# Hybrid decoder layer on one core: a turn between the gate rows' diagonal tiles and their matmul, three merged chunks turned on VectorE through DRAM, and read-backs issued by ScalarE

## The chip, the core and the metric

The kernel runs on one core of a Trainium2 chip. The metric is the device time of one execution in microseconds (us), here the median of several runs. The core has TensorE (PE, matmuls; its weight loads are listed apart as PEld), VectorE (DVE), ScalarE (ACT), GpSimd (POOL) and SyncE (SP), each with an instruction queue of its own that it works off in order. DMAs are issued from a queue and run beside the engines.

## What is computed

One layer of a decoder for 256 tokens of width 2048, all in float32:

```python
h = rmsnorm(x, ln_g);  proj = h @ w_in + b_in            # w_in: 2048 columns in, 14 groups of columns out
ml_out  = head_layernorm(mlstm(conv_silu(q,k), v, i, f)) * sigmoid(o) * silu(z)   # 6 heads
rt_out  = head_layernorm(retention(rope(q), rope(k), v)) * silu(z)                # 6 heads
xa_out  = softmax(q @ mk.T / 16) @ mv * silu(z)          # 4 heads, mk and mv from rmsnorm(mem) @ w_mem_kv
merged  = g0 * (ml_out @ w_br_ml) + g1 * (rt_out @ w_br_ret) + g2 * (xa_out @ w_br_xa)   # g = sigmoid(gate columns)
out     = rmsnorm(x + merged @ w_out, final_g)
```

The two gates `i` and `f` of the mLSTM (6 heads each) come from 12 columns of `w_in`. From them a small piece of work, called gate rows below, makes the running sums and maxima that the mLSTM needs.

## The kernel before

All weights pass once through the core in 1 MB tiles `raw` (128 x 2048), three buffers of them (`NRAW`), loaded by SP (`dma`, L212 to L239). Each half tile is a **unit**. For a unit ScalarE rounds the half to the matmul's reduced format (`wh`, L268) and VectorE takes the remainder (`wl`, L269); the products are three matmuls per block, high by high, high by low and low by high (L909 to L911), 12 matmuls of 512 columns in a unit. `wh` and `wl` have four buffers each (`NSPLIT`). The main loop (L932 to L944) writes, for each unit i: the splits up to unit i + 3 (`LA` = 3), the products of unit i, what is due at the end of a chunk of columns (`finish`), and then one turn of background work (`bg.step`, L125).

A cast for unit i + 3 therefore waits until PE has ended unit i - 1, whose buffer it takes, and PE needs it three units later.

**Background jobs** are Python generators. A `yield` ends a turn; `yield n` also lets the job rest for n further turns. Two jobs at most are begun, and awake ones take turns in rotation. The order that comes out is the program's order on each engine; nothing is scheduled at run time. So a turn's place is fixed by the number of yields ahead of it.

The places that the change touches:

- `gate_rows_job` (L384 to L444) begins after the 12 gate columns' products (L864, L865). Its first turn makes two 128 x 128 diagonal tiles on VectorE (L392) from the row norms, multiplies a tile of ones with each on PE (L393), which spreads the norms over all partitions, and copies the product (L395).
- `swapped` (L455 to L470) turns tiles of 128 x 512 by blocks: VectorE transposes 32 x 32 blocks (L463), four DMAs write the result to DRAM (L466), one DMA reads it back in the other order (L468), all issued by SP. Between write and read stands `yield 3`, between read and use `yield 2`. Users are `transposes_job` (10 times, two tiles, copy L476) and `out_transposes` (16 times, one tile, L526 to L531), 26 in all.
- `merge_job` (L699 to L713), one for each of four chunks of `merged`, transposes a chunk with eight 128 x 128 transposes on PE (L706) into two PSUM banks, from which ScalarE and VectorE make the high and low parts (L711, L712) that the output projection reads.

Of the kernel before, what the change touches and what calls it, by code (L numbers as in the profile page):

```python
# [12 lines left out]
ALU = mybir.AluOpType  # L13
# [3 lines left out]
P = 128  # L17
D = 2048
T = 256
# [131 lines left out]
def body(ctx, tc, A, out):  # L151
    nc = tc.nc
    V, S, G, PE = nc.vector, nc.scalar, nc.gpsimd, nc.tensor
# [6 lines left out]
    def til(tag, shape, dt=F32, bufs=1):  # L160
        names[tag] = names.get(tag, 0) + 1
        return sb.tile(shape, dt, tag=tag, name=f"{tag}_{names[tag]}", bufs=bufs)

    def bank(tag="bg", bufs=4):
        names[tag] = names.get(tag, 0) + 1
        return pp.tile([P, 512], F32, tag=tag, name=f"{tag}_{names[tag]}", bufs=bufs)

    def stage(w=512):
        return til("st", [P, 512], bufs=4)[:, :w]

    def f32(ap):
        return ap.bitcast(F32)
# [26 lines left out]
    ones = til("ones", [P, P])  # L199
# [48 lines left out]
    def part(w):  # L248
        off[0] += w
        return cst[:, off[0] - w:off[0]]  # L250
# [3 lines left out]
    bif, freq, ident, mask = part(1), part(64), part(P), part(P)  # L254
# [6 lines left out]
    rms = {n: til("r_" + n, [P, 2]) for n in ("mem", "x")}  # L261
# [122 lines left out]
    def gate_rows_job(psif):  # L384
        rows = iter(range(8))
        R = lambda: scr[:, next(rows), :]
        RT = R()
        G.memset(RT, 0.0)
        rb = bank()
        for tb in range(2):  # L390
            dg = stage(128)
            V.tensor_scalar(dg, ident, rms["x"][:, tb:tb + 1], None, op0=ALU.mult)  # L392
            PE.matmul(rb[:, tb * P:(tb + 1) * P], lhsT=ones, rhs=dg, start=True, stop=True)  # L393
        rbs = R()
        S.copy(rbs, rb[:, :T])  # L395
        fi = R()[:38]
        S.copy(fi, psif[64:102, :T])
        V.tensor_tensor(fi, fi, psif[:38, :T], op=ALU.add)
        V.tensor_tensor(fi, fi, rbs[:38], op=ALU.mult)
        V.tensor_scalar(fi, fi, bif[:38, 0:1], None, op0=ALU.add)  # L400
        yield
        f = fi[:6]
        ti = R()[:6]
        V.tensor_copy(ti, fi[32:38])
        e = R()[:6]
        V.scalar_tensor_tensor(e, f, -1.0, f, op0=ALU.mult, op1=ALU.max)
        S.activation(e, e, AF.Exp, bias=0.0, scale=-1.0)
        u = R()[:6]
        V.tensor_scalar(u, e, 1.0, None, op0=ALU.add)
        ln = R()[:6]  # L410
        S.activation(ln, u, AF.Ln)
        V.tensor_scalar(u, u, 1.0, None, op0=ALU.subtract)
        V.tensor_tensor(e, e, u, op=ALU.subtract)
        yield
        V.tensor_tensor(ln, ln, e, op=ALU.add)
        lf = u
        V.scalar_tensor_tensor(lf, f, 0.0, ln, op0=ALU.min, op1=ALU.subtract)
        b = R()[:6]
        for tb in range(2):
            sl = slice(tb * P, (tb + 1) * P)  # L420
            V.tensor_tensor_scan(b[:, sl], ones[:6], lf[:, sl], 0.0, op0=ALU.mult, op1=ALU.add)
        a = RT[:6]
        V.tensor_tensor(a, ti, b, op=ALU.subtract)
        yield
        zero = rbs
        G.memset(zero, 0.0)
        G.tensor_copy(MT, zero)
        V.tensor_tensor(sel, ident[:, 0:6], ident[:, 32:38], op=ALU.add)
        M = zero[:6]
        V.tensor_tensor_scan(M[:, :P], a[:, :P], a[:, :P], 0.0, op0=ALU.max, op1=ALU.max)  # L430
        mp = til("mp", [P, 1])[:6]
        V.tensor_tensor(mp, b[:, P - 1:P], M[:, P - 1:P], op=ALU.add)
        V.tensor_tensor_scan(M[:, P:], a[:, P:], a[:, P:], mp, op0=ALU.max, op1=ALU.max)
        V.tensor_scalar(RT[32:38, :P], a[:, :P], b[:, P - 1:P], None, op0=ALU.add)
        V.scalar_tensor_tensor(RT[64:70], b, -1.0, M, op0=ALU.mult, op1=ALU.subtract)
        V.tensor_copy(MT[:6], M)
        V.tensor_tensor(MT[32:38], M, f32(MT[:6]), op=ALU.subtract)
        yield
        ps = bank()
        for tb in range(2):  # L440
            PE.transpose(ps[:, tb * P:(tb + 1) * P], RT[:, tb * P:(tb + 1) * P], ident)
        S.copy(cT.rearrange("p a b -> p (a b)"), ps[:, :T])
        S.activation(enm, cT[:, :, 64:70], AF.Exp)
        yield  # L444
# [5 lines left out]
    outT = {}  # L450
# [4 lines left out]
    def swapped(us):  # L455

        n = len(us)
        x, y = (til(t, [P, 8 * P], bufs=2)[:, :4 * n * P].rearrange("p (a c) -> p a c", a=4) for t in ("tx", "ty"))  # L460
        d = dr.tile([4, 32, 4, n * P], F32, tag=f"td{n}", name=f"td{n}_{names['tx']}", bufs=2)
        for u in range(n):
            V.transpose(x[:, :, u * P:(u + 1) * P].rearrange("p b (c i) -> p c b i", i=32),  # L463
                        us[u].rearrange("p (c b j) -> p c b j", b=4, j=32))
        for a in range(4):
            nc.sync.dma_start(d.rearrange("b j a c -> a j b c")[a], x[32 * a:32 * a + 32])  # L466
        yield 3
        nc.sync.dma_start(y.rearrange("p a c -> p (a c)"), d.rearrange("b j a c -> (b j) (a c)"))  # L468
        yield 2
        return y  # L470

    def transposes_job(us, dst, off=0):

        yield
        y = yield from swapped(us)
        S.copy(dst[:, :, off:off + T].rearrange("p g (t a i) -> p g t a i", a=4, i=32),  # L476
               y.rearrange("p a (t g i) -> p g t a i", t=2, i=32))
        yield
# [39 lines left out]
    def out_transposes(o, h, g):  # L518

        y = yield from swapped([o])  # L520
        for db in range(2):
            k = 2 * h + db
            src = y.rearrange("p a (t d i) -> p d t a i", t=2, d=2)[:, db]
            hv, lv = (out_part(n, k)[:, 0].rearrange("p (t a i) -> p t a i", t=2, a=4) for n in "hl")
            if g is None:
                S.copy(hv, src)  # L526
                V.tensor_tensor(lv, src, f32(hv), op=ALU.subtract)
            else:
                S.activation(hv, src, AF.Copy, bias=0.0, scale=g[:, k:k + 1])
                for tb in range(2):  # L530
                    V.scalar_tensor_tensor(lv[:, tb], src[:, tb], g[:, k:k + 1], f32(hv)[:, tb],  # L531
                                           op0=ALU.mult, op1=ALU.subtract)
# [141 lines left out]
    merged = [None]  # L674
# [23 lines left out]

    def merge_job(c):  # L699

        yield
        us = [merged[0][:, c, tb, :] for tb in range(2)]
        ps = [bank(), bank()]
        for j in range(4):
            for tb in range(2):
                PE.transpose(ps[j // 2][:, (j % 2) * T + tb * P:(j % 2) * T + (tb + 1) * P],  # L706
                             us[tb][:, j * P:(j + 1) * P], ident)
        for i in range(2):
            h = outT["mh"][:, 4 * c + 2 * i:4 * c + 2 * i + 2, :].rearrange("p a t -> p (a t)")
            l = outT["ml"][:, 4 * c + 2 * i:4 * c + 2 * i + 2, :].rearrange("p a t -> p (a t)")  # L710
            S.copy(h, ps[i])  # L711
            V.tensor_tensor(l, ps[i], f32(h), op=ALU.subtract)  # L712
        yield  # L713
# [5 lines left out]
    def finish(ci, ps, bias, tbs=(0, 1)):  # L719
# [73 lines left out]
        elif kind == "br":  # L793
# [10 lines left out]
            if b == 1 and c:  # L804
                mjobs.append(bg.add(merge_job(c)))
# [45 lines left out]
    def products(i, u):  # L851
# [5 lines left out]
        if e[0] == "if":  # L857
            if hf == 0:
                psums[ci] = [bank()]
            ps = psums[ci][0]  # L860
            for k in range(8):
                kt = hf * 8 + k
                a = wh[:, k * P:(k + 1) * P]
                PE.matmul(ps[:, :T], lhsT=a, rhs=aTh[:, kt, :], start=kt == 0, stop=False)  # L864
                PE.matmul(ps[:, :T], lhsT=a, rhs=aTl[:, kt, :], start=False, stop=kt == NKT - 1)  # L865
            if hf == 1:
                jobs["rows",] = bg.add(gate_rows_job(ps))
            return
# [4 lines left out]
        if k0 == 0:  # L873
            load_bias(ci)
            if wname.startswith("w_br"):
                bg.finish(core_jobs[{"w_br_xa": "x", "w_br_ml": "m", "w_br_ret": "r"}[wname]])
            psums[ci] = [bank("d0", 2), bank("d1", 2)]
            if kind == "br" and idx == (1, 1):
                outT["mh"] = til("aTh", [P, NKT, T], F32R)
                outT["ml"] = til("aTl", [P, NKT, T], F32R)  # L880
                mjobs.append(bg.add(merge_job(0)))
# [151 lines left out]
```

## Time and profile before

| what | us |
|---|---|
| median of three runs | 1231.35 |
| lowest and highest run | 1230.87, 1232.48 |
| the profiled execution, its own time | 1233.26 |
| span of its instructions | 1231.3 |
| TensorE busy | 1217.9 (99%) |
| VectorE busy | 768.7 (62%) |
| ScalarE busy | 589.4 (48%) |
| GpSimd busy | 141.4 (11%) |

The page gives, from top to bottom, each engine's busy time, the span in 40 slices with the clock that TensorE was granted, the DMA queues, the chain of work that ended last, the costliest groups of instructions with the idle time ahead of them, and the DMA issues with their time to landing. TensorE has two levels of clock, 1.2 and 2.4 GHz; a granted clock of 1.00 is the upper one, 0.50 the lower. Ends of matmuls are modelled, so neighbouring matmuls overlap in the rows; the pace is read from the distance of their starts, which the chain of waits gives.

### The profile page before, as it was taken

Reading aid. Unit: us, or ns where it says so; the run is one execution under the profiler, and the core shown is the slowest. Engines: PE = TensorE matmul, PEld = TensorE weight load, DVE = VectorE, ACT = ScalarE, POOL = GpSimd, SP = SyncE. Lnnn points to the kernel's source line nnn. Section 1 sums busy time; section 2 is a strip of 40 time slices with the busy share of each in tenths; the row PEclk is TensorE's granted clock in tenths of the full one; section 3 lists DMA queues with packets and bytes.
Section 4 is the critical chain, followed back from the end, with each engine's and each line's share of the span. In section 5 each row is a group of like instructions: output and inputs, shape, how many; then the busy total and the mean of one; then the engine's idle time right before and its main releaser. Section 6 shows DMA issues by size and latency. Waiting matters only on the chain.

```text
span 1231.3 us, 14355 instructions
## 1 busy us (share of the span) xinstructions
PE 1217.9 (99%) x5516; PEld 1008.6 (82%) x5516; DVE 768.7 (62%) x988; ACT 589.4 (48%) x707; POOL 141.4 (11%) x164
## 2 busy tenths in 40 slices
PE   9999899999999999999999999999999999999997
PEld 7888788888888888888888888888888888888887
DVE  6564565545556676677687545666666865566554
ACT  6665444454434454455454543344444444444443
POOL 0005302800000030021021102101000000000101
PEclk9999899999999999999999999999999999999999
DMA  8986555746556647646756655575666657544752
GB/s 318 359 298 225 198 190 183 251 164 216 203 201 228 221 149 259 242 159 243 248 213 211 216 205 179 215 238 175 237 228 226 224 190 244 201 184 176 292 191 94
DMA packets 59828, 267.50 MB, mean 217 GB/s; under 512 B 6896, under 2 KB 20848, under 8 KB 31728
## 3 DMA queue, kind: packets, MB, share of 16 engines
q1 hardware_dynamic: 59328, 266.06, 61.0%
q8 instruction: 43, 0.70, 0.2%
q10 hardware_dynamic: 432, 0.53, 0.1%
q14 instruction: 25, 0.20, 0.0%
HBM read 255.03 MB, written 11.53 MB: 216 GB/s over the span
## 4 chain that ended last, share of the span: by engine, by line
PE 97%; issue 1%; DMA 1%; DVE 0%; SPq 0%; ACT 0%; POOLq 0%; POOL 0%; DVEq 0%; ACTq 0%
PE d L910 31%; PE d L909 31%; PE d L911 31%; DMA raw<-in_w_dram 1%; PE bg L511 1%; PE bg L486 1%; PE bg L596 0%; PE bg L598 0%; PE bg L597 0%; PE bg L706 0%; ACT wh L268 0%; PE bg L658 0%; PE bg L616 0%; PE bg L502 0%; SPq L226 0%
## 5 line engine op out<-in xcount | busy, mean ns | idle before, releaser
L269 DVE TENSOR_TENSOR wl<-raw,wh 128x1024 fp32r<-128x1024 f32 (+1 forms) x432 | 533.7, 1239 | 390.2 <-ACT wh L268 388.9
L268 ACT CAST wh<-raw 128x1024 fp32r<-128x1024 f32 (+1 forms) x432 | 444.7, 1033 | 493.3 <-PE d L911 459.0
L909 PE MATMUL d<-wh,aTh 128*128 128x512 f32 (+1 forms) x1344 | 523.3, 389 | 0.0
L910 PE MATMUL d<-wl,aTh 128*128 128x512 f32 (+1 forms) x1344 | 521.9, 388 | 0.0
L911 PE MATMUL d<-wh,aTl 128*128 128x512 f32 (+1 forms) x1344 | 517.8, 385 | 0.0
L909 PEld LDWEIGHTS d<-wh,aTh 128*128 128x128 f32 x1344 | 253.0, 188 | 53.6
L911 PEld LDWEIGHTS d<-wh,aTl 128*128 128x128 f32 x1344 | 252.9, 188 | 53.3
L910 PEld LDWEIGHTS d<-wl,aTh 128*128 128x128 f32 x1344 | 253.2, 188 | 49.4 <-DVE wl L269 0.3
L911 PE MATMUL d<-wh,oT 128*128 128x512 f32 x384 | 149.5, 389 | 0.0
L909 PE MATMUL d<-wh,oT 128*128 128x512 f32 x256 | 99.9, 390 | 0.0
L910 PE MATMUL d<-wl,oT 128*128 128x512 f32 x256 | 99.6, 389 | 0.0
L911 PEld LDWEIGHTS d<-wh,oT 128*128 128x128 f32 x384 | 72.1, 188 | 14.9
L683 POOL TENSOR_TENSOR gz<-gz,st 128x512 f32<-128x512 f32 x16 | 23.0, 1451 | 373.4 <-ACT gz L682 373.4
L910 PEld LDWEIGHTS d<-wl,oT 128*128 128x128 f32 x256 | 48.1, 188 | 9.9
L909 PEld LDWEIGHTS d<-wh,oT 128*128 128x128 f32 x256 | 48.1, 188 | 9.9
L909 PE MATMUL d<-wh,mgd 128*128 128x512 f32 x128 | 50.4, 394 | 0.8 <-ACT wh L268 0.8
L910 PE MATMUL d<-wl,mgd 128*128 128x512 f32 x128 | 50.3, 393 | 0.4 <-DVE wl L269 0.4
L816 POOL TENSOR_TENSOR oT<-oT,oT 128x512 f32<-128x512 f32 (+1 forms) x8 | 10.1, 1286 | 199.3 <-ACT st L814 199.3
L453 DVE SCALAR_TENSOR_TENSOR st<-d,r_x,bias 128x512 f32<-128x512 f32 x44 | 31.4, 744 | 0.0
L909 PEld LDWEIGHTS d<-wh,mgd 128*128 128x128 f32 x128 | 24.2, 189 | 6.6 <-ACT wh L268 1.7
L910 PEld LDWEIGHTS d<-wl,mgd 128*128 128x128 f32 x128 | 24.1, 188 | 6.4 <-DVE wl L269 1.6
L803 POOL TENSOR_TENSOR mgd<-mgd,gs 128x512 f32<-128x512 f32 x8 | 14.2, 1790 | 101.8 <-DVE gs L799 101.8
(188 smaller groups left out, 627.9 us busy)
## 6 DMA issues: line engine op xcount, KB each, us to landing
raw<-in_w_dram SPq DMA_DIRECT2D x209, 1024.0 KB, 4.8
bias<-in_bias_dram SPq DMA_DIRECT2D x37, 256.0 KB, 5.1
td<-tx SPq DMA_DIRECT2D x40, 128.0 KB, 4.4
ty<-td SPq DMA_DIRECT2D x10, 512.0 KB, 6.5
td<-tx SPq DMA_DIRECT2D x64, 64.0 KB, 2.9
ty<-td SPq DMA_DIRECT2D x16, 256.0 KB, 5.5
oT<-in_x_dram SPq DMA_DIRECT2D x3, 1024.0 KB, 6.9
raw<-in_w_dram SPq DMA_DIRECT2D x4, 512.0 KB, 8.1
```

The lines of the kernel that those rows point to most:

```text
L268: S.copy(wh, raw)
L269: V.tensor_tensor(wl, raw, f32(wh), op=ALU.subtract)
L453: V.scalar_tensor_tensor(dst, ps, r, bias, op0=ALU.mult, op1=ALU.add)
L486: PE.matmul(ps[:, tb * T:(tb + 1) * T], lhsT=qT[:, 2 * hh + db, tb * P:(tb + 1) * P], rhs=kT[:, 2 * hh + db, :], start=db == 0, stop=db == 1)
L511: PE.matmul(ps[:, tb * T:(tb + 1) * T], lhsT=pT[:, c:c + P], rhs=v[:, mb, hh * T:(hh + 1) * T], start=mb == 0, stop=mb == 1)
L683: G.tensor_tensor(dst, dst, zu, op=ALU.mult)
L803: e.tensor_tensor(m[:, c, tb, :], m[:, c, tb, :], t[:, tb, :], op=ALU.add)
L816: G.tensor_tensor(y, y, g[:, c0:c0 + W], op=ALU.mult)
L909: PE.matmul(ps, lhsT=h, rhs=a, start=kt == 0, stop=False)
L910: PE.matmul(ps, lhsT=h, rhs=b, start=False, stop=False)
L911: PE.matmul(ps, lhsT=l, rhs=a, start=False, stop=kt == nk - 1)
```

## The change

Three edits. The diagonal tiles are made in the gate rows' first turn, in the job's own rows of the tile `gs` instead of staging tiles; the matmul, now one of 256 columns, stands in the next turn. In `swapped` the read-back is issued by ScalarE's queue instead of SP's, and both rests are one turn shorter. The first three of the four chunks of `merged` use `swapped` instead of PE transposes; the fourth is left as it was.

```diff
     def gate_rows_job(psif):
...
         G.memset(RT, 0.0)
+        dg = R()
+        for tb in range(2):
+            V.tensor_scalar(dg[:, tb * P:(tb + 1) * P], ident, rms["x"][:, tb:tb + 1], None, op0=ALU.mult)
+        yield
         rb = bank()
-        for tb in range(2):
-            dg = stage(128)
-            V.tensor_scalar(dg, ident, rms["x"][:, tb:tb + 1], None, op0=ALU.mult)
-            PE.matmul(rb[:, tb * P:(tb + 1) * P], lhsT=ones, rhs=dg, start=True, stop=True)
-        rbs = R()
+        PE.matmul(rb[:, :T], lhsT=ones, rhs=dg, start=True, stop=True)
+        rbs = dg
         S.copy(rbs, rb[:, :T])
...
     def swapped(us):
...
-        yield 3
-        nc.sync.dma_start(y.rearrange("p a c -> p (a c)"), d.rearrange("b j a c -> (b j) (a c)"))
         yield 2
+        S.dma_start(y.rearrange("p a c -> p (a c)"), d.rearrange("b j a c -> (b j) (a c)"))
+        yield 1
         return y
...
     def merge_job(c):
 
-        yield
         us = [merged[0][:, c, tb, :] for tb in range(2)]
+        if c < 3:
+            y = yield from swapped(us)
+            for tb in range(2):
+                src = y.rearrange("p a (t g i) -> p t g a i", t=2, i=32)[:, tb]
+                h, l = (outT[n][:, 4 * c:4 * c + 4, tb * P:(tb + 1) * P].rearrange("p g (a i) -> p g a i", i=32)
+                        for n in ("mh", "ml"))
+                S.copy(h, src)
+                V.tensor_tensor(l, src, f32(h), op=ALU.subtract)
+            return
+        yield
         ps = [bank(), bank()]
```

How instructions move, at three places. Line numbers after the change are 1 to 10 higher: L469 is the read-back, L477 the copy of the user, L394 the gate rows' matmul, L919 to L921 the products. Names end in a running number.

**TensorE, behind the gate columns' products, before:** the two small matmuls stand ahead of the next unit.

```order
L864 MATMUL bg_1158<-aTh_111,wh_1110 128x256
L865 MATMUL bg_1158<-aTl_112,wh_1110 128x256
L393 MATMUL bg_1207<-st_1208,ones_68 128x128
L393 MATMUL bg_1207<-st_1211,ones_68 128x128
L909 MATMUL d_7_1227<-wh_1135,aTh_111 128x512
L910 MATMUL d_7_1227<-wl_1136,aTh_111 128x512
```

**And after the change:** the next unit follows the products at once,

```order
L874 MATMUL bg_1166<-aTh_111,wh_1118 128x256
L875 MATMUL bg_1166<-aTl_112,wh_1118 128x256
L919 MATMUL d_7_1223<-wh_1143,aTh_111 128x512
L920 MATMUL d_7_1223<-wl_1144,aTh_111 128x512
L921 MATMUL d_7_1223<-wh_1143,aTl_112 128x512
```

and the matmul stands four units later, between the fourth and the fifth:

```order
L920 MATMUL d_7_1224<-wl_1216,aTh_111 128x512
L921 MATMUL d_7_1224<-wh_1215,aTl_112 128x512
L394 MATMUL bg_1303<-gs_87,ones_68 128x256
L919 MATMUL d_7_1223<-wh_1240,aTh_111 128x512
L920 MATMUL d_7_1223<-wl_1241,aTh_111 128x512
```

The diagonal tiles themselves (L391) move behind the remainder `wl_1216` of that fourth unit on VectorE.

**ScalarE, first read-back of the program (keys of the cross-attention), before:** SP issues it, and ScalarE only has the copy, L476.

```order
L268 CAST wh_510<-raw_407 128x1024
L264 ACTIVATE aTh_111<-oT_1_88,cst_109 128x256 x2
L268 CAST wh_530<-raw_407 128x1024
L264 ACTIVATE aTh_111<-oT_1_88,cst_109 128x256 x2
L268 CAST wh_553<-raw_447 128x1024
L264 ACTIVATE aTh_111<-oT_1_88,cst_109 128x256 x2
L268 CAST wh_573<-raw_447 128x1024
L264 ACTIVATE aTh_111<-oT_1_88,cst_109 128x256 x2
L268 CAST wh_595<-raw_491 128x1024
L476 COPY k_442<-ty_463 128x1024
```

**And after the change:**

```order
L268 CAST wh_510<-raw_407 128x1024
L469 DMA ty_463<-td_1_464 128x1024
L264 ACTIVATE aTh_111<-oT_1_88,cst_109 128x256 x2
L268 CAST wh_531<-raw_407 128x1024
L264 ACTIVATE aTh_111<-oT_1_88,cst_109 128x256 x2
L268 CAST wh_553<-raw_447 128x1024
L477 COPY k_442<-ty_463 128x1024
L264 ACTIVATE aTh_111<-oT_1_88,cst_109 128x256 x2
L268 CAST wh_574<-raw_447 128x1024
```

The read-back stands three casts behind the transposes, and the copy, with two casts between, two units earlier than before.

**VectorE, the block transposes of the second pair of mLSTM heads (L464), after the change:** they follow two evacuations (L454) and two remainders of the values (L269, `vl`).

```order
L269 TENSOR_TENSOR wl_3676<-raw_3561,wh_3675 128x1024
L454 SCALAR_TENSOR_TENSOR st_3700<-d_22_3507,r_x_116,bias_3505 128x512
L269 TENSOR_TENSOR vl_3698<-st_3700,v_3697 128x512
L454 SCALAR_TENSOR_TENSOR st_3704<-d_22_3508,r_x_116,bias_3505 128x512
L269 TENSOR_TENSOR vl_3698<-st_3704,v_3697 128x512
L464 STREAM_TRANSPOSE tx_3708<-st_3521 128x4x4x32
L464 STREAM_TRANSPOSE tx_3708<-st_3522 128x4x4x32
L269 TENSOR_TENSOR wl_3718<-raw_3596,wh_3717 128x1024
```

The same bundle stands so at the third pair of mLSTM heads and at the second and third pair of retention heads.

## Rows read from the trace of the kernel before

**Rows 1.** Page, part 4: the chain that ended last, share of the span by engine.
```profile
PE 97%; issue 1%; DMA 1%; DVE 0%; SPq 0%; ACT 0%; POOLq 0%; POOL 0%; DVEq 0%; ACTq 0%
```
**Rows 2.** Who waited for whom, TensorE's waits: us in total, times, longest.
```profile
PE bg L393 <- DVE st L392: 3.8, 1, 3.8
PE bg L206 <- POOL nhalf L202: 1.0, 1, 1.0
```
**Rows 3.** Timeline, 136 to 158 us: start, us, instruction [idle before, releaser].
```profile
143.02 0.28 PE L865 MATMUL bg<-aTl,wh 128*128 128x256 f32 x1
...
144.83 2.02 DVE L269 TENSOR_TENSOR wl<-raw,wh 128x1024 fp32r<-128x1024 f32 x1 [1.63 <-ACT wh L268]
...
146.78 0.47 DVE L392 TENSOR_SCALAR st<-cst,r_x 128x128 f32<-128x128 f32 x2
...
147.11 1.22 PE L393 MATMUL bg<-st,ones 128*128 128x128 f32 x4 [3.81 <-DVE st L392]
```
**Rows 4.** Stretches: us, busy of PE, PEld, DVE, ACT, POOL; clock; DMA share, GB/s.
```profile
144.00:148.00 4.00, 0.89 (x5) 0.90 (x5) 2.42 (x3) 0.80 (x1) 2.02 (x3) 0.76 0.49 205
148.00:153.00 5.00, 5.00 (x14) 3.94 (x14) 3.36 (x6) 3.30 (x5) 2.60 (x4) 0.51 0.17 25
...
1090.00:1140.00 50.00, 50.00 (x234) 41.53 (x233) 31.84 (x36) 21.19 (x24) 0.00 (x0) 1.00 0.50 180
```
**Rows 5.** Chain in order of time, 136 to 160 us: start, us, what.
```profile
147.11 1.22 PE bg L393 x4
148.33 0.43 PE d L909
...
153.01 0.23 PE d L911
```
**Rows 6.** Chain in order of time, around 438 and around 1094 us.
```profile
438.32 0.43 PE bg L616 x2
...
1093.76 0.88 PE bg L706 x8
```
**Rows 7.** Groups by line and shape, TensorE: busy us, mean ns | idle before.
```profile
L706 PE MATMUL bg<-cst,mgd 128*128 128x128 f32 x32 | 4.1, 272 | 0.0
```
**Rows 8.** Page, part 5: the split of weights; busy, mean ns | idle, what ended it.
```profile
L269 DVE TENSOR_TENSOR wl<-raw,wh 128x1024 fp32r<-128x1024 f32 (+1 forms) x432 | 533.7, 1239 | 390.2 <-ACT wh L268 388.9
L268 ACT CAST wh<-raw 128x1024 fp32r<-128x1024 f32 (+1 forms) x432 | 444.7, 1033 | 493.3 <-PE d L911 459.0
```
**Rows 9.** One line of the program, its read-backs (L468), all 26.
```profile
DMA to landing us min/median/max: 4.8/5.8/9.0
```
**Rows 10.** Timeline of VectorE around the second pair of retention heads.
```profile
885.29 1.22 DVE L269 TENSOR_TENSOR wl<-raw,wh 128x1024 fp32r<-128x1024 f32 x1
...
889.89 0.69 DVE L269 TENSOR_TENSOR vl<-st,v 128x512 fp32r<-128x512 f32 x1 [0.69 <-ACT v L268]
...
894.77 1.30 DVE L463 STREAM_TRANSPOSE tx<-st 128x512 f32<-128x512 f32 x2
```
**Rows 11.** The four writes (L466) behind that transpose, 896 to 898 us.
```profile
L466 SPq DMA_DIRECT2D td<-tx x4: 325/430/457, 896.1 to 897.4; - x4
...
DMA to landing us min/median/max: 4.9/5.2/5.3
```
**Rows 12.** Timeline of ScalarE at the first read-back's place after the change.
```profile
54.82 1.05 ACT L268 CAST wh<-raw 128x1024 fp32r<-128x1024 f32 x1 [0.51 <-PE d L911]
```
**Rows 13.** The first four writes (L466), 50 to 53 us.
```profile
L466 SPq DMA_DIRECT2D td<-tx x4: 334/440/1212, 50.2 to 52.3; - x4
...
DMA to landing us min/median/max: 7.8/8.5/8.9
```
**Rows 14.** One line of the program, L833: its two issues on ScalarE, in ns.
```profile
L833 ACTq DMA_DIRECT2D out_dram<-oT x2: 338/341/344, 1221.1 to 1226.7; - x2
```
**Rows 15.** Page, part 6: DMA issues, KB each, median us to landing.
```profile
out_dram<-oT SPq DMA_DIRECT2D x6, 256.0 KB, 2.9
...
out_dram<-oT ACTq DMA_DIRECT2D x2, 256.0 KB, 2.5
```

More of the change, by code (lines that the diff above doesn't have):

```diff
@@ L699, in merge_job @@
     def merge_job(c):
+        us = [merged[0][:, c, tb, :] for tb in range(2)]
+        if c < 3:
[7 more added lines that the diff above has]
+            return
         yield
-        us = [merged[0][:, c, tb, :] for tb in range(2)]
         ps = [bank(), bank()]
```

## Prediction

> **What bounds the kernel now.** I read the chain of waits first: 97% of the span lies on TensorE [rows 1]. So a microsecond off TensorE's path is a microsecond off the time, and work on any other engine counts only where TensorE comes to wait for it. The list of waits says where it does: once for 3.8 us, for the diagonal tiles of the gate rows; the next longest is 1.0 us at the start of the program [rows 2]. The timeline shows why. PE's last gate product starts at 143.02, and the small matmul starts at 147.11 after 3.81 us of idleness, because VectorE first works off a remainder until 146.85 and only then makes the tiles, at 146.78 to 147.25 [rows 3]. The table of stretches shows what the hole leaves behind: the granted clock averages 0.76 and then 0.51, so it has fallen to the lower level, 1.2 GHz, when PE resumes [rows 4]. In the chain, the products from 148.33 to 153.01 take 0.43 us each where they take 0.23 afterwards [rows 5].
>
> **The diagonal tiles' turn.** The next unit now follows the gate products at once, and the matmul stands four units on. Three terms, all on TensorE's path:
>
> - The hole: 3.81 us [rows 3].
> - The slow clock: from 148.33 to 153.01 are 4.68 us for 11 products [rows 5]. At 12 products in a unit of 2.75 us, 0.229 each, they take 2.52. Gain 2.16 us.
> - The small matmul: two of 128 columns at the lower level take 1.22 us [rows 5]. One of 256 columns in float32 at the upper level is the pair of L616, 0.43 us [rows 6]. Gain 0.79 us.
>
> Together 6.76 us. This needs work for PE during the hole, and it is there: the program runs three units ahead in its splits, so of the units behind the gate columns the first two were split before 143, and the third has its remainder at 146.85 [rows 3], while PE wants it two units on, after 143.1 + 5.5 = 148.6. The tiles now stand one remainder later on VectorE, PE wants them after four units, about 154, and 147.25 is what they were made at before. The cover is ample. That the gate rows' later turns shift by some units costs nothing: their results are used by the mLSTM's heads, 80 units on.
>
> **The three chunks.** Eight transposes of a chunk take 0.88 us of the chain [rows 6]; three chunks give 2.63 us (the middle one reads 0.87). Here a rule stands against the row. The rows give 0.11 us per transpose on the path, though the mean length of one is 272 ns [rows 7], since each starts before the one ahead has ended. The Trainium skill (TensorE: Matmul & The Clock Gate, Part 4) puts one PE transpose inside a kernel at about 275 ns; by it 24 would cost 6.6 us and the gain would be 4 us larger. The trace agrees with that length but not with its use as a pace, and I keep 2.63.
>
> What is put in their place: six block transposes on VectorE, two per chunk at 1.30 us the pair [rows 10], 3.9 us in a stretch where VectorE works 31.84 of 50 us [rows 4]; copies and remainders as before, read from SBUF; twelve writes and three reads, 3 MB, where the DMA engines are half busy [rows 4]. SP gives up 26 reads and gets 12 writes. The last of the three chunks is ready about five units before the output projection reads it. None of this is on the path: cost nothing. Were the cover gone, the output projection would wait for the chunk.
>
> **The read-backs on ScalarE.** This is the cost. A DMA issue of ScalarE takes 0.34 us [rows 14]; 29 are 9.9 us of an engine that idles 459.0 us waiting for PE [rows 8]. But the issue waits until the four writes have landed, the copy two units later waits until the read has landed, and the casts of the weights queue behind both. Cover: a cast is released three units, 8.25 us, before PE wants its unit; cast and remainder take 1.03 + 1.24 [rows 8], which leaves 5.9 us. So lateness up to 5.9 us costs nothing. Two kinds of places come near it.
>
> *Behind a bundle.* At the second and third pairs of the mLSTM and of the retention heads the transposes follow two evacuations and two remainders. From the start of the remainder ahead of such a bundle to its end are 5.29 us (885.29 to 890.58), then 1.30 of transposes [rows 10]: 6.6 us. ScalarE reaches the read 8.25 us after that start, 1.65 us after the transposes end. The writes start at 896.1, as the transposes end, and the last, issued at 897.4, lands some 5.2 later [rows 11], 6.5 us after the end. So ScalarE stands 4.9 us. The read lands 5.8 later at the median [rows 9]; the copy and the next cast follow, about 1.05 each: 4.9 + 5.8 + 2.1 = 12.8 us, where the cast was due at 8.25. Late by 4.55, within 5.9, margin 1.35 us. With the slowest landing, 9.0 [rows 9], it is 3.2 more and PE waits 1.85 us. Four such places.
>
> *At the start,* where the DMA engines are fullest: ScalarE reaches the first read at 54.82 + 1.05 = 55.87 [rows 12]; the last write is issued at 52.3 and lands 7.8 later at the earliest, 60.1 [rows 13]. It stands 4.3 us. Then come the read's 5.8, the copy and two pieces of other work that are in the queue anyway; I make the margin 1.0 us. With 9.0 PE waits 2.2 us.
>
> At the other 24 the transposes end 4 us earlier against the casts, and the margin is larger by that.
>
> So the cost lies between nothing (median landings, all margins hold) and 4 x 1.85 + 2.2 = 9.6 us (slowest landings everywhere); below nothing is excluded, since SP was on no path. I take 1.0 us, near the lower end: half of one such wait, because 9.0 is one of 26. Another row speaks for still less: the same 256 KB lands in 2.5 us from ScalarE's queue and in 2.9 from SP's [rows 15], so reads that no longer stand behind a weight tile in SP's queue may land sooner, and the cost be nothing. Against it, the Trainium skill (DMA: Bandwidth & Descriptors, Issuing engines are not separate DMA queues) says that DMAs of all issuing engines run on the same 16 DMA engines and that a second issuer saves issue time alone; by it landings stay where they are. The two rows differ in the skill's disfavour, but stem from the program's idle end.
>
> **Sum.** 6.76 + 2.63 - 1.0 = 8.4 us. The profiled execution took 1233.26 us for a span of 1231.3, so it would take 1224.9. The median of the runs shown lies 1.9 us lower, at 1231.35; from there 1223.0 us.
>
> **Rivals.**
>
> *Slow read-backs.* Landings at the five near places are at the slow end. Up to 9.6 us of waits leave 9.4 - 9.6, no gain: 1231.6. For it: two write groups that landed late [rows 11, 13]. Against: 5.8 as the median. Halfway lie 1226 to 1228.
>
> *Slower: the clock falls again at those waits.* The hole at 147 cost more than its length: 2.16 + 0.79 us of half clock. If waits of about 2 us at the five places each let the clock fall to 1.2 GHz and cost some 2.5 us besides, that is 9.6 + 12.5 = 22.1 against 9.4: 1244.0. It turns slower than before once the waits with their clock exceed 9.4 us: three such places do it. Against: it takes slow landings first, and the only fall in this trace came with 3.8 us of idleness.
>
> *The hole moves.* The change does not do what it says: PE runs into another wait behind the gate columns, such as the third unit's remainder or the cross-attention's first scores, which now stand there after three units and need ScalarE's copy. If the 6.76 us come back in full, 2.63 remain: 1228.7. Against: each was ready some microseconds ahead by the working above.
>
> **How the numbers follow.** Forecast, with waits of 0 to 3 us (1221.9 to 1225): 0.72. Slow read-backs: 0.16, of which 0.12 lie between 1225 and 1228.8 and 0.04 at or above. The hole moves: 0.06, on the edge. Slower: 0.06. The range 1221.2 to 1227.5 takes in the full gain of 9.4 with the runs' scatter, 1231.35 being 0.5 above the lowest run, and the nearer part of the slow read-backs; it leaves about 0.17 out. A measurement of this kernel can tell about 0.2%, 2.5 us, from no change. Faster by more than that, below 1228.9: 0.72 + 0.12 + 0.04 of the moved hole = 0.88. Within 0.2%: 0.06. Slower: 0.06.
>
> **What would show it.** Right: no wait of PE at L394, granted clock 1.00 from 140 to 160 us, eight transposes left (L716) in place of 32, ScalarE waiting for DMA at L469 by 3 to 5 us at the start and at the four bundles, and PE's waits for `wh` and `wl` in all under 3 us. Wrong: a wait of PE at L919 or L920 behind a read-back, a second fall of the clock, or a hole behind the gate columns under another name.

## The result, and the profile after

| | before | after |
|---|---|---|
| median, us | 1231.81 (4 runs, 1230.87 to 1232.48) | 1222.90 (4 runs, 1222.77 to 1223.45) |
| the profiled execution, its own time | 1233.26 | 1222.77 |
| span of its instructions | 1231.3 | 1220.8 |
| TensorE busy | 1217.9 | 1211.3 |
| ScalarE busy | 589.4 | 585.9 |
| VectorE busy | 768.7 | 759.4 |

The change is faster: 8.9 us off the median, ratio 0.9929 with a 95% interval of 0.9912 to 0.9946. The forecast was 1223.0 us, in a range of 1221.2 to 1227.5.

The page's chain that ended last, by engine, is a little more TensorE's than it was [rows 1]:

```profile
PE 98%; DMA 1%; issue 0%; SPq 0%; DVE 0%; ACT 0%; POOLq 0%; POOL 0%; DVEq 0%; ACTq 0%
```

TensorE's waits after the change (us in total, times, longest) answer to [rows 2]. The wait for the diagonal tiles is gone, and nothing has come in its place. The two waits for `wh` and `wl` lie at 5 to 10 us, at the program's start; from there until the output's tail at 1215 us no idle time of TensorE over 0.15 us is left in the trace.

```profile
PE bg L206 <- POOL nhalf L202: 1.0, 1, 1.0
PE d L919 <- ACT wh L268: 0.6, 2, 0.4
PE d L920 <- DVE wl L269: 0.4, 2, 0.2
```

The table of stretches (us; busy of PE, PEld, DVE, ACT, POOL with counts; granted clock; DMA share, GB/s) shows the place of the former hole [rows 4]: PE is busy throughout and its clock stays at the upper level.

```profile
140.00:144.00 4.00, 4.00 (x28) 3.69 (x28) 2.36 (x4) 3.32 (x5) 1.68 (x2) 1.00 0.62 214
144.00:148.00 4.00, 4.00 (x18) 3.22 (x18) 4.00 (x5) 2.69 (x3) 3.70 (x6) 1.00 0.24 98
148.00:153.00 5.00, 5.00 (x24) 4.17 (x23) 2.58 (x3) 1.05 (x1) 3.63 (x5) 1.00 0.90 310
```

In the chain in order of time (start, us, what), the small matmul of 256 columns stands behind a unit and takes 0.43 us, where the pair of 128 took 1.22 at the low clock [rows 5]. The products around it take 0.23 each. One group of eight transposes is left, at 0.88 us, where there were four [rows 6].

```profile
155.00 0.23 PE d L921
155.23 0.43 PE bg L394 x2
155.66 0.23 PE d L919
...
1129.51 0.88 PE bg L716 x8
```

ScalarE now waits for the turns through DRAM, which it hardly did. Its list before (us in total, times, longest) had 2.7 us for the reads in two rows, and none for the writes:

```profile
ACT oT L529 <- DMA ty<-td: 2.0, 1, 2.0
...
ACT k L476 <- DMA ty<-td: 0.7, 1, 0.7
```

After the change it has:

```profile
ACT wh L268 <- PE d L921: 426.8, 276, 4.3
ACT wh L268 <- DMA td<-tx: 20.3, 6, 5.6
...
ACT oT L530 <- DMA ty<-td: 10.1, 4, 4.1
...
ACT k L477 <- DMA ty<-td: 6.6, 4, 2.9
...
ACT aTh L264 <- DMA td<-tx: 4.3, 1, 4.3
```

It still idles 426.8 us for TensorE, 459.0 before [rows 8]. What it waits for the writes (`td<-tx`) and for the reads (`ty<-td`), 41.3 us in these four rows alone, it takes from time that it had to spare.

To place the gain, I cut each trace at two points: the first product of the 46th unit (130 to 131 us) and that of the 101st (301 to 309), then on to that of the 416th (1188 to 1200). Stretch A, 46th to 101st, holds the gate rows; its other work on TensorE is the same in all kernels but e4 and e12. Stretch B, 101st to 416th, holds 18 of the 26 read-backs of the kernel before, 21 of the 29 after, and the chunks of `merged`.

| kernel | stretch A, us | stretch B, us |
|---|---|---|
| before | 177.95 | 889.40 |
| after | 171.33 | 886.42 |
| e1, gate turn alone | 172.97 | 889.29 |
| e2, three chunks alone | 176.87 | 886.61 |
| e3, read-backs alone | 173.73 | 889.19 |
| e4, hole filled | 175.31 | 889.33 |
| e5, change without read-backs | 172.93 | 886.57 |
| e6, change without gate turn | 173.72 | 886.48 |
| e7, reads issued by SP | 171.33 | 886.44 |
| e8, transposes twice | 176.87 | 892.88 |
| e9, gate turn later | 171.39 | 886.56 |
| e10, rest shorter | 171.25 | 887.71 |
| e11, four chunks | 171.35 | 886.05 |
| e12, attention too | 171.79 | 886.71 |

Between the two profiled executions A gives 6.62 us and B 2.98; another 0.97 us lies ahead of A, where TensorE has the same work and the start (131.13 against 130.16 us) differs from execution to execution: over the kernels of the table it ranges from 130.16 to 131.34. The profile of before is also one in which the clock stayed low for longer than in two others with the same hole, by about 1 us of time (e4 below). These two things go the way in which the spans differ by more (10.5 us) than the medians (8.9).

### The profile page after: what moved, and what is told of

Its sections match the earlier page's. It is cut to its first block, busy times and chain, and to the rows that moved or that the text cites. A ratio compares the mean times of both kernels' runs of the same rounds, so it can differ in the third digit from the quotient of the medians.

```text
span 1220.8 us, 14373 instructions
## 1 busy us (share of the span) xinstructions
PE 1211.3 (99%) x5490; PEld 1003.3 (82%) x5490; DVE 759.4 (62%) x994; ACT 585.9 (48%) x705; POOL 142.7 (12%) x164
## 4 chain that ended last, share of the span: by engine, by line
PE 98%; DMA 1%; issue 0%; SPq 0%; DVE 0%; ACT 0%; POOLq 0%; POOL 0%; DVEq 0%; ACTq 0%
PE d L920 32%; PE d L919 31%; PE d L921 31%; PE bg L512 1%; PE bg L487 1%; DMA raw<-in_w_dram 1%; PE bg L597 0%; PE bg L599 0%; PE bg L598 0%; PE bg L659 0%; PE bg L617 0%; PE bg L875 0%; PE bg L874 0%; PE bg L503 0%; SPq L226 0%
## 5 line engine op out<-in xcount | busy, mean ns | idle before, releaser
L269 DVE TENSOR_TENSOR wl<-raw,wh 128x1024 fp32r<-128x1024 f32 (+1 forms) x432 | 528.3, 1229 | 388.7 <-ACT wh L268 388.0
L268 ACT CAST wh<-raw 128x1024 fp32r<-128x1024 f32 (+1 forms) x432 | 443.6, 1033 | 484.1 <-PE d L921 426.8
L919 PE MATMUL d<-wh,aTh 128*128 128x512 f32 (+1 forms) x1344 | 522.4, 389 | 0.0
L921 PE MATMUL d<-wh,aTl 128*128 128x512 f32 (+1 forms) x1344 | 516.8, 385 | 0.0
L919 PEld LDWEIGHTS d<-wh,aTh 128*128 128x128 f32 x1344 | 252.4, 188 | 54.0
L921 PEld LDWEIGHTS d<-wh,aTl 128*128 128x128 f32 x1344 | 252.4, 188 | 53.1
L921 PE MATMUL d<-wh,oT 128*128 128x512 f32 x384 | 149.4, 389 | 0.0
L919 PE MATMUL d<-wh,oT 128*128 128x512 f32 x256 | 99.6, 389 | 0.0
L921 PEld LDWEIGHTS d<-wh,oT 128*128 128x128 f32 x384 | 72.1, 188 | 14.9
L919 PEld LDWEIGHTS d<-wh,oT 128*128 128x128 f32 x256 | 48.0, 188 | 10.0
L919 PE MATMUL d<-wh,mgd 128*128 128x512 f32 x128 | 50.1, 391 | 0.6 <-ACT wh L268 0.6
L553 POOL TENSOR_TENSOR k<-k,gs 128x1024 f32<-128x1024 f32 x3 | 7.4, 2465 | 212.7 <-ACT k L551 212.7
L454 DVE SCALAR_TENSOR_TENSOR st<-d,r_x,bias 128x512 f32<-128x512 f32 x44 | 31.4, 745 | 0.0
L919 PEld LDWEIGHTS d<-wh,mgd 128*128 128x128 f32 x128 | 24.0, 188 | 6.1 <-ACT wh L268 1.2
```

What stands on the lines that cost most here:

```text
L268: S.copy(wh, raw)
L269: V.tensor_tensor(wl, raw, f32(wh), op=ALU.subtract)
L454: V.scalar_tensor_tensor(dst, ps, r, bias, op0=ALU.mult, op1=ALU.add)
L553: G.tensor_tensor(qf, qf, yf, op=ALU.mult)
L919: PE.matmul(ps, lhsT=h, rhs=a, start=kt == 0, stop=False)
L921: PE.matmul(ps, lhsT=l, rhs=a, start=False, stop=kt == nk - 1)
```

## The experiments

### The three edits one by one (e1, e2, e3)

e1 is the kernel before with the first hunk of the diff alone,

```diff
+        yield
         rb = bank()
...
+        PE.matmul(rb[:, :T], lhsT=ones, rhs=dg, start=True, stop=True)
```

e2 with the third alone,

```diff
+        if c < 3:
+            y = yield from swapped(us)
...
+            return
+        yield
```

and e3 with the second alone:

```diff
-        yield 3
-        nc.sync.dma_start(y.rearrange("p a c -> p (a c)"), d.rearrange("b j a c -> (b j) (a c)"))
         yield 2
+        S.dma_start(y.rearrange("p a c -> p (a c)"), d.rearrange("b j a c -> (b j) (a c)"))
+        yield 1
```

> The kernel before with the gate rows' turn alone. My theory: 6.76 us less than the kernel before (hole 3.81, slow clock 2.16, small matmul 0.79), granted clock 1.00 from 140 to 160 us and no wait of PE at the small matmul. Rival (the hole moves): less than 3 us gained, a wait of PE of 2 us or more behind the gate columns under another name.

> The kernel before with the three chunks turned on VectorE through DRAM alone, read-backs from SP's queue with the old rests. My theory: 2.63 us less, eight L706 transposes left on PE, no wait of PE for the chunks at the output projection. Rival by the length of one transpose (272 ns): 6.5 us less. Rival (the chunks come late): no gain or a loss, PE waiting at the output projection's first products.

> The kernel before with ScalarE's read-backs and the shorter rests alone. My theory: within 1 us of the kernel before, ScalarE's waits for DMA behind writes 3 to 5 us at the start and behind the bundles, covered by the 5.9 us. Rival (slow read-backs): 3 us or more slower, with waits of PE for the weights' halves.

Against the kernel before on the same chip (1232.03 us):

| | median, us | ratio | gain, us |
|---|---|---|---|
| e1, gate turn | 1227.59 | 0.9964 (0.9952 to 0.9976) | 4.4 |
| e2, three chunks | 1229.42 | 0.9982 (0.9974 to 0.9991) | 2.6 |
| e3, read-backs | 1228.31 | 0.9970 (0.9958 to 0.9981) | 3.7 |

e2 is as expected. e1 falls short by 2.4 us, and e3, for which a small cost was expected, is a gain. Together they make 10.7, more than the whole change: two of them claim the same microseconds. TensorE's waits say which. In e1:

```profile
PE bg L394 <- DVE gs L391: 1.3, 1, 1.3
```

and in e3:

```profile
PE bg L393 <- DVE st L392: 2.2, 1, 2.2
```

The order of e1's instructions shows the reason. With the old rests, the turn that follows the tiles' turn comes not four units later but one:

```
L912 MATMUL d_7_1218<-wh_1135,aTl_112 128x512
L394 MATMUL bg_1231<-gs_87,ones_68 128x256
L910 MATMUL d_7_1217<-wh_1152,aTh_111 128x512
```

`wh_1135` is the first unit behind the gate columns, `wh_1152` the second. On the timeline of VectorE and PE in e1 (start, us, instruction, idle before and releaser), the tiles are made at 146.73, as late as before [rows 3], and PE reaches the matmul 1.27 us too early:

```profile
144.72 2.09 DVE L269 TENSOR_TENSOR wl<-raw,wh 128x1024 fp32r<-128x1024 f32 x1 [1.64 <-ACT wh L268]
146.73 0.47 DVE L391 TENSOR_SCALAR gs<-cst,r_x 128x128 f32<-128x128 f32 x2
...
147.26 0.70 PE L394 MATMUL bg<-gs,ones 128*128 128x256 f32 x2 [1.27 <-DVE gs L391]
```

In e3 nothing of the gate rows was edited. But the shorter rests of the jobs ahead of it move the rotation of turns, and the gate rows' first turn now falls one unit later: PE has a unit to do, and the hole shrinks from 3.8 to 2.2 us. After so short a hole the clock did not fall (e3, stretches):

```profile
144.00:148.00 4.00, 1.78 (x11) 1.21 (x10) 3.55 (x4) 1.78 (x2) 1.19 (x2) 1.00 0.25 107
148.00:153.00 5.00, 5.00 (x25) 4.10 (x24) 3.45 (x5) 2.75 (x4) 2.85 (x4) 1.00 0.76 264
```

Stretch B agrees: e3 takes 889.19 us there, and the kernel before 889.40. Over the 315 units that hold 18 of the read-backs the edit is worth 0.2 us; its gain is in stretch A, at the hole.

### The hole filled with idle work (e4)

Sixteen matmuls of the ones tile with itself stand ahead of the gate rows' matmul in the kernel before; their results are not used.

```diff
         rb = bank()
+        for _ in range(16):
+            PE.matmul(rb[:, :P], lhsT=ones, rhs=ones, start=True, stop=True)
```

> The kernel before, its order as it is, with 16 idle matmuls of ones on ones (128 columns, 0.22 us each at the upper clock, 3.5 us in all) put on TensorE into the hole ahead of the gate rows' small matmuls. The hole of 3.81 us stays as lost time, but PE is not idle in it. My theory: the clock stays at 1.00 and the clock's share of the sum, 2.16 and the larger part of 0.79, comes back: 2.6 to 3.0 us less than the kernel before. Rival (the slow products at 148 to 153 us are due to something else, such as the weights' loads): the products after the hole still take 0.43 us and the time is that of the kernel before or longer.

Measured: 1229.84 us, ratio 0.9981 (0.9973 to 0.9990), a gain of 2.2 us. The tiles come as late as before, and PE ends its idle work 0.3 us ahead of them; but with PE at work in the hole, the clock stays up (e4, stretches):

```profile
144.00:148.00 4.00, 3.75 (x30) 3.42 (x29) 2.44 (x3) 0.90 (x3) 1.59 (x3) 1.00 0.37 156
148.00:153.00 5.00, 5.00 (x24) 4.09 (x23) 3.70 (x7) 3.68 (x5) 3.36 (x6) 1.00 0.18 44
```

So the clock has a share of its own in what the hole cost, beside the idle time, and this is shown and not only argued. Its size by the medians, 2.2 us, is a little under the expected 2.6 to 3.0. The profile of e2, with the same hole of 3.8 us, tells why: there the clock is low for a shorter time than in the profile of before, which read 0.76 and 0.51 [rows 4].

```profile
144.00:148.00 4.00, 1.40 (x7) 1.22 (x8) 2.42 (x3) 0.92 (x3) 1.52 (x3) 0.91 0.39 164
148.00:153.00 5.00, 5.00 (x18) 3.98 (x17) 3.70 (x7) 3.68 (x5) 3.43 (x7) 0.73 0.24 62
```

With the lower level at 0.50, the means of the two stretches make about 6.8 us at that level in the profile of before and 3.4 in e2. Stretch A is 176.87 us in e2, and the same in e8 below, against 177.95 in the profile of before. What a fall costs thus differs by about 1 us between executions of the same instructions: stretch A of e4 is 2.64 us below the profile of before and 1.56 below e2.

### The change without one of its parts (e5, e6), and with the gate turn moved by hand (e9)

e5 is the change with the old `swapped` (the hunk of e3 taken back), e6 the change with the old gate turn. e9 is e5 with one edit more:

```diff
             V.tensor_scalar(dg[:, tb * P:(tb + 1) * P], ident, rms["x"][:, tb:tb + 1], None, op0=ALU.mult)
-        yield
+        yield 1
         rb = bank()
```

> The change without its read-back edit (gate turn and three chunks alone; reads issued by SP, rests 3 and 2). Theory 'shared hole': gate and read-back edits both act on the one hole behind the gate columns, so the parts that were measured singly add up: -4.4 and -2.6 us, 1225.0 us, 2.1 above the whole change, with a wait of TensorE at the small matmul (L394) of about 1.3 us and no other new wait. Rival 'own worth': the read-back edit's 3.7 us of the run alone lie elsewhere in the program; then 1226.6 us, with no wait at L394 or with waits of TensorE elsewhere that the change does not have. By the prediction's own terms (6.76 and 2.63, read-backs a cost) it would be 1222 us.

> The change without its gate edit (three chunks and read-back edit alone; diagonal tiles made in the turn of the matmul). Theory 'shared hole': -2.6 and -3.7 us, 1225.7 us, TensorE's wait at L393 about 2.2 us, clock 1.00 or down for less than the 6.8 us of before. Rival 'own worth': the gate turn's 4.4 us of the run alone are missing in full: 1227.3 us. By the prediction's 6.76 it would be 1229.7 us, with 3.8 us of wait at L393.

> The change without its read-back edit, and with the gate rows' matmul two units later (the first yield made a yield 1, which puts it behind the third unit after the gate columns instead of the first). Theory 'place of the turn': all that the read-back edit was worth is that it moved this turn; the 1.3 us wait at L394 goes, and the time is that of the whole change, 1222.9 to 1223.4 us, with the reads on SP and the long rests. Rival: the read-backs are worth something of their own, and 1225 us stays although the wait is gone.

e5 took 1225.12 us, ratio 0.9943 (0.9930 to 0.9955), 2.2 us above the change, where "shared hole" expected 1225.0, and has this wait again:

```profile
PE bg L394 <- DVE gs L391: 1.3, 1, 1.3
```

e9 took 1223.46 us, ratio 0.9932 (0.9919 to 0.9944). It has no wait at L394, stretch A is 171.39 us (171.33 in the change) and B 886.56 (886.42). With SP issuing the reads and with the long rests, all but 0.6 us of the gain is there, once the gate rows' matmul stands two units later. This decides for the theory of the place: the read-back edit was worth what it did to the rotation of turns.

e6 took 1226.97 us, ratio 0.9958 (0.9945 to 0.9970), between the two theories (1225.7 and 1227.3) and nearer to the rival's; the median alone does not decide. Its wait is the 2.2 us that "shared hole" named, as in e3:

```profile
PE bg L393 <- DVE st L392: 2.2, 1, 2.2
```

Stretch A is 2.4 us longer than in the change, B alike (886.48). The medians differ by 4.1. Of the other 1.7 us the profiled execution of e6 shows 1.2 ahead of stretch A (131.34 against 130.16), where TensorE has the same work; whether that is the scatter of the start or belongs to this kernel stays open.

### Which queue issues the reads, and how long the rest is (e7, e10)

e7 is the change with SP's queue, e10 the change with ScalarE's queue and a still shorter rest:

```diff
-        S.dma_start(y.rearrange("p a c -> p (a c)"), d.rearrange("b j a c -> (b j) (a c)"))
+        nc.sync.dma_start(y.rearrange("p a c -> p (a c)"), d.rearrange("b j a c -> (b j) (a c)"))
```

```diff
-        yield 2
+        yield 1
         S.dma_start(y.rearrange("p a c -> p (a c)"), d.rearrange("b j a c -> (b j) (a c)"))
```

> The change with its shorter rests, the reads issued by SP in place of ScalarE. Theory 'the rests decide': the queue is worth nothing by itself, 1222.9 us within 1 us; SP stands in its read until the writes have landed, but weight tiles are asked for early enough; the landings of the 512 KB reads rise from 4.7 us at the median to about 6.5 as in the kernel before, since they share a queue with weight tiles. Rival 'the queue decides': SP stands 4 to 5 us at 29 reads with the weight loads queued behind, raw tiles come late, and TensorE waits for weights by 2 us or more in sum: above 1225 us.

> The change with the rest ahead of the read one turn shorter still (yield 1 in place of yield 2), so that ScalarE reaches each read 2.75 us earlier, and the writes land no earlier. Theory 'thin cover': ScalarE stands 2.75 us longer at most reads; the places where the change left 0.4 to 2.4 us between a remainder's end and TensorE's use of it run out, and TensorE waits by 3 to 7 us in sum: 1226 to 1230 us. Rival 'ample cover': within 1 us of the change, 1222 to 1224 us.

e7: 1223.27 us, ratio 0.9930 (0.9918 to 0.9943), within 0.4 us of the change, with stretches A and B as in the change. ScalarE's waits for writes are gone from the list; its copies wait longer for the reads instead (e7, ScalarE's waits; 10.1 and 6.6 us in the change):

```profile
ACT oT L530 <- DMA ty<-td: 20.5, 10, 6.3
ACT k L477 <- DMA ty<-td: 13.1, 4, 4.3
```

The issuing queue is thus worth nothing here. The reads of 512 KB landed in 5.5 us at the median in e7, 4.7 in the change, 6.5 before (the pages' last part, of e7, of the change and of before):

```profile
ty<-td SPq DMA_DIRECT2D x13, 512.0 KB, 5.5
ty<-td SPq DMA_DIRECT2D x16, 256.0 KB, 6.0
```

```profile
ty<-td ACTq DMA_DIRECT2D x13, 512.0 KB, 4.7
...
ty<-td ACTq DMA_DIRECT2D x16, 256.0 KB, 5.4
```

```profile
ty<-td SPq DMA_DIRECT2D x10, 512.0 KB, 6.5
...
ty<-td SPq DMA_DIRECT2D x16, 256.0 KB, 5.5
```

e10: 1225.80 us (1223.94 to 1226.52), ratio 0.9949 (0.9937 to 0.9962), 2.9 us above the change: "thin cover" in direction, just below its 1226 to 1230 us in size. The list of ScalarE's waits shows the predicted lengthening, the longest from 5.6 to 8.2 us and the sum from 20.3 to 41.8:

```profile
ACT wh L268 <- DMA td<-tx: 41.8, 10, 8.2
```

TensorE waits for late weights at 61.7 us by 0.28 and at 648.5 by 0.44 (VectorE's remainder behind ScalarE's cast); in the change it had no such wait behind the start:

```profile
648.51 0.50 PE L920 MATMUL d<-wl,aTh 128*128 128x512 f32 x1 [0.44 <-DVE wl L269]
```

That execution was the fastest of its five; the others took about 2 us more, and have no profile. That they wait at the same places for longer is argued, not shown.

### What a transpose costs on the path (e8)

The kernel before, with each of the eight transposes of a chunk made twice:

```diff
-        for j in range(4):
+        for j in (0, 1, 2, 3, 0, 1, 2, 3):
             for tb in range(2):
```

> The kernel before with its 32 merged transposes on TensorE made twice. Theory 'pace': 0.11 us each on the path, 32 x 0.11 = 3.5 us more, 1235.5 us. Rival 'length': 272 ns each, 8.7 us more, 1240.7 us.

Measured: 1235.12 us, ratio 1.0026 (1.0017 to 1.0036), 3.2 us more for 32 transposes, 0.10 each. In the chain sixteen of them take twice what eight took:

```profile
1092.23 1.75 PE bg L706 x16
```

The pace decides, not the 272 ns of one [rows 7]. Stretch B agrees: 892.88 us against 889.40 are 3.48 for 32, 0.11 each.

### More of the same: the fourth chunk (e11) and the attention's probabilities (e12)

```diff
-        if c < 3:
+        if c < 4:
             y = yield from swapped(us)
```

```diff
-        ps = bank()
-        for tb in range(2):
-            for mb in range(2):
-                c = (tb * 2 + mb) * P
-                PE.transpose(ps[:, c:c + P], pr[:, tb * T + mb * P:tb * T + (mb + 1) * P], ident)
+        y = yield from swapped([pr])
         pT = til("core", [P, 512], bufs=4)
-        S.copy(pT, ps)
+        S.copy(pT.rearrange("p (g a i) -> p g a i", a=4, i=32), y.rearrange("p a (g i) -> p g a i", i=32))
```

> The change with the fourth chunk of merged turned through DRAM too. It saves eight more transposes, 0.88 us. Theory: the fourth chunk is made last, and the output projection comes to it before its way through DRAM ends; TensorE waits there by about 3.7 us and the clock falls once more: about 1228 us. Rival: the output projection reads it late enough, 1222.0 us.

> The change, and the 16 transposes of the cross-attention's probabilities (L502 before) also by blocks through DRAM, four heads with one tile each. Theory 'pace': 16 x 0.11 = 1.76 us off TensorE's path, 1221.1 us, no new wait of TensorE. Rival: four more reads among units whose weights have 0.4 to 2 us of cover make TensorE wait as much as is saved: 1223 us or more.

e11: 1221.79 us (1220.96 to 1222.37), ratio 0.9918 (0.9904 to 0.9931). My theory fell, the rival holds: the median is 1.1 us below the change's, and the two sets of runs do not touch, though the two ratios' intervals overlap. In the two profiles the last 26 units of stretch B, where the transposes were, are 0.79 us shorter (71.43 against 72.22), which is the expected gain. The matmuls of 256 columns at the program's end gain about as much again (1.36 us for twelve of them, against 1.41), and some units around 660 us lose about 0.3; why, no run shows. The chunk is ready exactly when it is wanted. In its timeline the read is issued at 1134.86 and the copy begins at 1140.06:

```profile
1134.86 0.33 ACTq L469 DMA_DIRECT2D ty<-td  x1
...
1140.06 1.14 ACT L709 CAST aTh<-ty 128x512 fp32r<-128x512 f32 x2 [0.32 <-DMA ty<-td]
```

and TensorE's weight queue waits 0.2 us for the remainder (L710), TensorE itself not at all. There is no margin left here, and it is the fastest kernel of this study.

e12: 1225.93 us (1223.65 to 1228.03), ratio 0.9954 (0.9940 to 0.9967), 3.0 us above the change. The rival's time came (1223 us or more), by another wait than the one it named. The transposes' time is saved, and a new wait takes it back: stretch A is 171.79 us, 0.46 above the change with 1.97 of wait in it. Each head of the cross-attention now goes through DRAM twice. Before the first product with `w_br_xa` the program makes all turns that these jobs still have, one after another, and the last head now has its second way through DRAM left: between its read and its copy stands no cast. The copy waits 7.1 us, and the products wait for the copy (e12, timeline):

```profile
295.99 0.33 ACTq L469 DMA_DIRECT2D ty<-td  x1
298.69 0.71 ACT L523 CAST oT<-ty 128x256 fp32r<-128x256 f32 x2 [7.11 <-DMA ty<-td]
...
299.14 0.50 PE L915 MATMUL d<-wh,oT 128*128 128x512 f32 x1 [1.97 <-ACT oT L523]
```

These 2.0 us are the whole of TensorE's idle time after the start in that execution, again the fastest of five; what the slower ones lose besides has no profile.

## Why the prediction was right, point by point

- **The hole, 3.81 us:** gone in full, with no wait of TensorE in its place, as predicted.
- **The slow clock, 2.16 us:** the mechanism is shown by e4. Its size was read from one execution, which had one of the longer falls. The three terms of the gate rows made 6.76 us; stretch A gives 6.62 against the profile of before, but 5.54 against e2 and e8 (176.87 - 171.33), which have the same hole.
- **The small matmul, 0.79 us:** 1.22 us became the predicted 0.43.
- **The three chunks, 2.63 us:** e2 measured 2.6, stretch B 2.8 (889.40 - 886.61), and e8 confirmed the pace of 0.11 us against the length. The Trainium skill (TensorE: Matmul & The Clock Gate, Part 4) gives 275 ns for one transpose of 128 x 128 in bf16 inside a kernel; an estimate that takes this figure for the cost of each of e8's 32 would be 8.8 us. e8 lost 3.2, and the measurement decides; the length of one here, 272 ns in float32, agrees with the page's.
- **The read-backs, a cost of 1.0 us:** nothing; TensorE waits 1.0 us in all for `wh` and `wl`, all of it in the program's first 10 us. Here the term was mis-sized, and it stayed within its bounds of 0 and 9.6. At the start ScalarE stood 4.31 us, the 4.3 of the prediction:

```profile
53.86 1.05 ACT L268 CAST wh<-raw 128x1024 fp32r<-128x1024 f32 x1 [0.51 <-PE d L921]
...
58.84 0.33 ACTq L469 DMA_DIRECT2D ty<-td  x1
59.22 0.91 ACT L264 ACTIVATE aTh<-oT,cst 128x256 fp32r<-128x256 f32 x2 [4.31 <-DMA td<-tx]
```

At the bundle of the second pair of retention heads it stood 2.72 us in place of 4.9, since the writes landed sooner than the 5.2 us after issue that [rows 11] had:

```profile
882.29 1.30 DVE L464 STREAM_TRANSPOSE tx<-st 128x512 f32<-128x512 f32 x2
...
887.62 0.33 ACTq L469 DMA_DIRECT2D ty<-td  x1
888.05 1.05 ACT L268 CAST wh<-raw 128x1024 fp32r<-128x1024 f32 x1 [2.72 <-DMA td<-tx]
```

The four writes between these rows (L467):

```profile
DMA to landing us min/median/max: 2.3/2.6/2.8
```

At two more of the four bundles the wait was 2.74 and 2.55 us (573.8 and 957.3); at the fourth, at 483.9, the list puts 4.26 us down to TensorE. So the predicted 3 to 5 us of waiting for DMA came at the start, and less at three of the bundles. The thinnest cover behind a read-back was at none of the five places that I had listed. It is where two heads' outputs are turned in successive turns, and where ScalarE waits for the writes and then for the reads:

```profile
646.35 1.05 ACT L268 CAST wh<-raw 128x1024 fp32r<-128x1024 f32 x1 [5.64 <-DMA td<-tx]
...
652.66 0.91 ACT L530 ACTIVATE oT<-ty,cst 128x256 fp32r<-128x256 f32 x2 [4.10 <-DMA ty<-td]
...
654.54 1.23 DVE L269 TENSOR_TENSOR wl<-raw,wh 128x1024 fp32r<-128x1024 f32 x1 [0.20 <-ACT wh L268]
```

That remainder ends at 655.77, and TensorE takes it at 656.16: 0.39 us to spare, and 0.16 to the weight load of that product at 655.93. e10 went over this edge. The kernel before had no more to spare at another place, among the mLSTM's jobs, where the weight load waited for the remainder and TensorE lost less than 0.1 us:

```profile
561.16 0.19 PEld L910 LDWEIGHTS d<-wl,aTh 128*128 128x128 f32 x1 [0.35 <-DVE wl L269]
```

- **The sum:** 8.4 us predicted, 8.9 measured. Two errors of about 1 us cancel. The gate rows' terms were too large by 1.2 us for an execution with the shorter fall (6.76 against 5.54), and the read-backs cost 1.0 less; with B's 2.98 us in place of 2.63 the stretches make 5.54 + 2.98 = 8.5. The remaining 0.4 us is within what single executions scatter by ahead of stretch A. That the forecast of 1223.0 us met the median to 0.1 us is luck: besides these errors, the median of before that it started from, 1231.35, became 1231.81 with a fourth run.
- **What the prediction had wrong in its working** was who earns what. It wrote the 6.76 us to the gate edit and called the read-back edit a cost. The gate edit alone gives 4.4, since with the old rests its matmul stands only one unit behind the gate products and meets the late tiles; the four units that the prediction read from the order come from both edits. e9 shows that the rests are worth that shift and no more, e7 that ScalarE's queue is worth nothing.
- **The rivals:** slow read-backs did not come, nor a second fall of the clock; the hole that moves is what e1, e5 and e6 have, each with a part of the change missing.

## What to carry to other kernels

Where an order is written by turns, every rest that is lengthened or shortened moves other jobs' turns. Before an edit is credited with a gain, look up in the order of the changed program where each late turn now stands, and undo the edits one at a time: gains that add up to more than the whole share a place.

A gap on the engine that bounds costs its length and may cost more in the clock after it; e4 measures the second part by filling the gap, 2.2 us for a gap of 3.8. And a wait that has been moved to an engine with idle time is free only as far as its cover goes: here the cover was used up to 0.4 us or less, one rest shorter lost 2.9 us, and one more use of the same trick (e12) gave back more than it saved, while another (e11) paid in full.

## What the runs showed that I had not expected

- Holes of 1.3 us (e1, e5) and 2.2 us (e3, e6) left the granted clock at 1.00; after the hole of 3.8 us it fell in every profile (before, e2, e8), for a time that differed: the stretch from 148 to 153 us had a mean of 0.51 in the profile of before, 0.73 in e2 and 0.71 in e8.
- The first 45 units, with the same work for TensorE in all kernels, ended between 130.16 and 131.34 us in the profiles, with waits for weights in the first 15 us that came and went. Differences of a microsecond between single spans mean nothing here; stretches cut behind the start agree to 0.1 us (171.33, 171.33, 171.35 in stretch A of the change, e7 and e11).
- A turn through DRAM that ended so late that the weight queue waited 0.2 us for it (e11, one profile) left TensorE without a wait, and none of the four runs was above 1222.37 us.
